# Head gates packed into three recurrent weight tiles, and two groups of steps placed a chunk later

## The chip, the cores and the metric

The kernel runs on one core of one Trainium2 chip. The metric is device microseconds of one launch, all weights being read from HBM; the median of three runs before the change is 1436.12 us (1435.93 to 1438.66).

## The reference

Two layers of a first block (hybrid mixer, memory cross attention, convolutional feed-forward) and then one layer of a second block run over 256 tokens of width 1024, in fp32. The change touches the second block alone, in its first part:

```python
xn = rmsnorm(x, norm_mix)
(u_rnn, u_gate, q, k_c, v_c, k_s, v_s, k_w, v_w, g_nsa, g_a, g_b) = jnp.split(xn @ w_in, cuts, axis=-1)
h_a = rg_lru(causal_depthwise_conv(u_rnn, conv_w, conv_b), gate_a_w, ...)   # 1344 channels, 4 gate blocks of 336
y_a = h_a * jax.nn.gelu(u_gate, approximate=True)
y_b = nsa_mixer(q, k_c, v_c, k_s, v_s, k_w, v_w, g_nsa, ...)
#   kc = rmsnorm(compress_blocks(k_c)); vc = compress_blocks(v_c)   (pe added, then gelu(flat @ w1) @ w2)
#   gates = sigmoid(g_nsa): 16 heads x 3;  o = g0 * o_c + g1 * o_s + g2 * o_w
merged = sigmoid(g_a) * (y_a @ proj_a) + sigmoid(g_b) * (y_b @ proj_b)
h = x + merged @ w_out
return h + square(relu(rmsnorm(h, norm_mlp) @ w_mlp_in)) @ w_mlp_out
```

`g_nsa` is a product of the 1024 features with 48 columns. `u_rnn` and `u_gate` have 1344 columns each.

## The kernel before, in words

Activations lie feature-major in SBUF: `fmh` and `fml` hold the high and the low part of an fp32 value, split so that a product runs as three fp32r matmuls (high by high, low by high, high by low). A weight tile is one DMA of up to 128x1024 elements into `raw`; ScalarE casts it to `wh` (L220) and VectorE subtracts for `wl` (L221). `Stream.take` hands out the tiles in a fixed order (`order2`), issues loads ahead on SP's queue, and splits two tiles ahead; tiles named `pkv` are used as they are, unsplit. There are four `raw` buffers and four of each of `wh` and `wl`.

A chunk is one weight tile. `mm_a` multiplies its eight 128-row parts with the 256 tokens: 24 matmuls (L410 to L412) into one PSUM tile of pool `mm`, which has four. The recurrent stage (`lru_steps`) walks four blocks: three chunks `ur` of 112 output columns with a convolution after each (kind "u"), three of `ug` with a gelu (kind "g"), and the block's two gates `lga` and `lgx`, each one tile with three groups of nine matmuls, 27 in all (kind "b"). After the two gates of a block, `lru_tail` does the scan in five pieces.

The order on TensorE is the program's order. On the other engines a scheduler lays out the instructions with priorities; each engine then runs its queue in order. Work beside the chunks is tied to ticks: every `take` is a tick (`tick`, L349), `later(n, fn)` runs a function n ticks on, and generators in `back` go one step a tick.

Around the change, `block2` first makes the queries and the keys `k2` and `v2`. `put_ks` (L1533) turns the normalised keys of two token halves, two kinds each, by four transposes into a PSUM tile of pool `tp`, which has two; ScalarE and VectorE split the result into `ks` (L1529, L1530). Then come four chunks `cc`, whose results are copied alternately by ScalarE and VectorE into two tiles `zt` (L1555) and completed by a sum with the position values (L1557, on VectorE). Then the chunk `gn`, the head gates, with its 48 columns padded to 128; ScalarE copies it out (L1562), and two ticks later `gates` transposes it (L1567).

The compressed keys are `phi_steps`: eight `pkv` steps, one between any two recurrent chunks, each with eight fp32 matmuls on both `zt` tiles (L1215); then, one step a tick, a gelu, transposes, copies, a second product, a norm (`kc_ss`, `rstd` on GpSimd, L1254) and a transpose (L1258). After the last, `nsa_units` starts: 16 attention units with score matmuls, VectorE reductions (L1398 to L1411), six ScalarE exponentials (L1417), transposes and sums, the first four units five ticks apart and the others two. They run beside the recurrent blocks and the merge gates `ga`, `pa`, `gb`.

Of the kernel before, what the change touches and what calls it, by code (L numbers as in the profile page):

```python
# [15 lines left out]
AF = mybir.ActivationFunctionType  # L16
# [3 lines left out]
S = 256  # L20
D = 1024
# [5 lines left out]
RW = 112  # L27
# [105 lines left out]
def layout2(f, o):  # L133
    g = {k[:-2]: v[0] for k, v in f.items() if k.endswith("_2") and v.ndim > 1 and v.shape[0] == 1}
    w = g["w_in"]
    cut = np.cumsum([0, 1344, 1344, 1024] + [256] * 6 + [48, 1024, 1024])
    ur, ug, q, kc, vc, ks, vs, kw, vw, gn, ga, gb = (w[:, i:j] for i, j in zip(cut[:-1], cut[1:]))
    o["ur"], o["ug"] = pack_a(ur, RW), pack_a(ug, RW)
    o["q2"] = pack_b(q)
    o["k2"] = pack_b(np.concatenate([ks, kw], 1))  # L140
    o["v2"] = pack_b(np.concatenate([vs, vw], 1))
    o["cc"] = pack_a(np.concatenate([kc, vc], 1))
    o["gn"] = pack_a(np.pad(gn.reshape(D, 16, 3)[:, :, [1, 2, 0]].transpose(0, 2, 1).reshape(D, 48), ((0, 0), (0, 80))))
    o["ga"], o["gb"] = pack_a(ga), pack_a(gb)
    for key, name in (("lga", "gate_a_w"), ("lgx", "gate_x_w")):
        o[key] = np.concatenate([pack_a(g[name][b], RW, RW, 9) for b in range(4)])
    o["pa"] = pack_a(g["proj_a"], 128, RW, 6)
    o["pb"] = pack_a(g["proj_b"])
    o["wo2"] = pack_b(g["w_out"])
    o["minb"], o["min"] = pack_b(g["w_mlp_in"][:, :512]), pack_a(g["w_mlp_in"][:, 512:])  # L150
    o["mout"] = pack_b(g["w_mlp_out"])
    w1 = np.stack([g[n].reshape(8, 2, 128, 256) for n in ("phi_k_w1", "phi_v_w1")], 1)
    o["pkv"] = np.ascontiguousarray(w1.transpose(0, 3, 1, 2, 4).reshape(8, 128, 1024))
    w2 = np.stack([g["phi_k_w2"], g["phi_v_w2"]])
    o["phi2"] = np.ascontiguousarray(w2.reshape(2, 2, 128, 64).transpose(2, 0, 1, 3))
    pe = [g[n].reshape(16, 2, 64).transpose(1, 2, 0).reshape(128, 16) for n in ("phi_k_pe", "phi_v_pe")]
    two = [np.tile(g[n], 2)[:, None] for n in ("q_norm", "ks_norm", "kw_norm")]
    o["feat2"] = np.ascontiguousarray(np.concatenate(two + pe, 1))
    o["rnn"] = np.ascontiguousarray(np.concatenate(
        [feat(g["conv_w"], RW).reshape(RW, -1)] + [feat(g[n].reshape(-1), RW) for n in  # L160
                                                   ("conv_b", "gate_a_b", "gate_x_b", "lru_lambda")], 1))
    o["kcg"] = g["kc_norm"]
    o["nmix"], o["nmlp"] = g["norm_mix"], g["norm_mlp"]
    rb = np.concatenate([f["rel_bias_2"], np.full((1, 16), NEG, np.float32)])
    p = np.arange(128)[:, None]
    dist = 128 + p - np.arange(256)[None]
    idx = np.where(dist >= 0, _bucket(dist), 32)
    o["tbias"] = np.ascontiguousarray(rb[idx].transpose(0, 2, 1))
    dc = p[:, :, None] + 128 * np.arange(2)[None, :, None] - (16 * np.arange(15) + 31)[None, None]
    o["cbias"] = np.ascontiguousarray(rb[np.where(dc >= 0, _bucket(dc), 32)].transpose(0, 1, 3, 2))  # L170
    o["cval"] = (p >= 31).astype(np.float32)
# [84 lines left out]
class Program:  # L256
# [50 lines left out]

    def order2(self, add):
        add("q2", len(EARLY))
        for key in ("k2", "v2", "cc", "gn"):  # L310
            add(key)
        n = 0
        for kind, b in LRU_ORDER:
            for i in range(2 if kind == "b" else 3):
                if kind == "b":
                    add("lgx" if i else "lga", b, b + 1)
                else:
                    add("ur" if kind == "u" else "ug", 3 * b + i, 3 * b + i + 1)
                if n < 8:
                    add("pkv", n, n + 1)  # L320
                n += 1
        for key in ("ga", "pa", "gb", "pb", "wo2", "minb", "min", "mout"):
            add(key)
# [955 lines left out]
        nc.vector.scalar_tensor_tensor(cl, cl, -4.0, sr, op0=OP.mult, op1=OP.add)  # L1279
        nc.vector.tensor_scalar(rp[:, 5 * RT:7 * RT], rp[:, 5 * RT:7 * RT], 0.5, None, op0=OP.mult)  # L1280

    def lru_steps(self, xs, ya, pool, prm):


        nc, w = self.nc, self.w
        cw, cb, ba, bx, cl = prm
        xcs = {}
        for kind, b in LRU_ORDER:
            if kind == "u":
                xc = xcs[b] = pool.tile([RW, 3, S], F32, name="xc", bufs=2)  # L1290
                for i in range(3):
                    n = 3 * b + i
                    ps = self.mm((128, S))
                    self.mm_a(ps[:RW], w.take("ur"), self.fmk(xs), nw=RW)
                    nc.scalar.activation(xc[:, i], ps[:RW], AF.Identity, bias=cb[:, n:n + 1],
                                         scale=cw[:, 3 * RT + n:3 * RT + n + 1])
                    for s in (1, 2, 3):
                        nc.vector.scalar_tensor_tensor(xc[:, i, s:], ps[:RW, :S - s],
                                                       cw[:, (3 - s) * RT + n:(3 - s) * RT + n + 1], xc[:, i, s:],
                                                       op0=OP.mult, op1=OP.add)  # L1300
                    yield
                xh = pool.tile([RW, 3, S], F32R, name="xch", bufs=1)
                xl = pool.tile([RW, 3, S], F32R, name="xcl", bufs=1)
                self.split(xh, xl, xc)
                continue
            if kind == "g":
                ug = self.yp.tile([RW, 3, S], F32, name="ug", tag=f"yah{b}", bufs=1)
                for i in range(3):
                    ps = self.mm((128, S))
# [165 lines left out]
    def block2(self, x, xs, outs):  # L1475
        nc, tc, w, a = self.nc, self.tc, self.w, self.a
        with ExitStack() as st:
# [54 lines left out]

            def put_ks(t, kn):  # L1533
                for i in range(2):
                    self.later(2 + i, partial(put_k, kn, t, i))

            self.spawn(self.head_norm([out.rearrange("p (h d) -> p h d", d=64) for out in outs], 8, self.sm, put_ks,
                                      True))
# [4 lines left out]
            for kind in range(2):  # L1543
# [12 lines left out]
                pe = fp[:, 3 + 16 * kind:19 + 16 * kind]  # L1556
                nc.vector.tensor_add(zt, zt, pe[:, :, None].to_broadcast([128, 16, 60]))  # L1557
                zts.append(zt)
            ps = self.mm((128, S))
            self.mm_a(ps, w.take("gn"), self.fmk(xs))  # L1560
            gs = self.k2((48, S))
            nc.scalar.copy(gs, ps[:48])  # L1562

            def gates():
                for t in range(2):
                    tp = self.tp((128, 48))
                    nc.tensor.transpose(tp, gs[:, t * 128:t * 128 + 128], self.ident[:48, :48])  # L1567
                    gv = gt[:, t].rearrange("p b h -> p (b h)")
                    nc.scalar.activation(gv, tp, AF.Tanh, scale=0.5)
                    nc.vector.tensor_scalar(gv, gv, 0.5, 0.5, op0=OP.mult, op1=OP.add)  # L1570
                nc.vector.tensor_scalar(gt[:, 0, 2], gt[:, 0, 2], cval, None, op0=OP.mult)

            self.later(2, gates)

            ya, self.yp = [], pool
            yb = self.fm()
# [3 lines left out]
            self.back.append(self.attend(self.nsa_units(qt, ks, v, vcz, gt, pcs, yb), *NSA))  # L1580
            with tc.tile_pool(name="lru", bufs=1) as lp:
                prm = rp[:, :4 * RT], rp[:, 4 * RT:5 * RT], rp[:, 5 * RT:6 * RT], rp[:, 6 * RT:7 * RT], cl
                for i, _ in enumerate(self.lru_steps(xs, ya, lp, prm)):
                    if i < 8:
                        next(phi)
                    elif i == 8:
                        self.back.append(phi)
                for g in self.back:
                    if g.gi_code.co_name == "lru_tail":
# [92 lines left out]
```

## Time and profile before

| what | us |
|---|---|
| median of three runs | 1436.12 |
| profiled execution | 1439.39 |
| its span, first to last instruction | 1437.6 |
| TensorE busy | 1415.7 (98%) |
| VectorE busy | 1083.4 (75%) |
| ScalarE busy | 891.7 (62%) |

Matmuls are pipelined: their recorded durations overlap, and what one costs in a row of equal ones is the distance between two starts. A wait is a gap before an instruction, put down to what ended it. Line numbers are those of the kernel before; in the changed file the same lines stand 2 to 10 lines further down.

### The profile page before, as it was taken

Reading aid. Unit: us, or ns where it says so; the run is one execution under the profiler, and the core shown is the slowest. Engines: PE = TensorE matmul, PEld = TensorE weight load, DVE = VectorE, ACT = ScalarE, POOL = GpSimd, SP = SyncE. Lnnn points to the kernel's source line nnn. Section 1 sums busy time; section 2 is a strip of 40 time slices with the busy share of each in tenths; the row PEclk is TensorE's granted clock in tenths of the full one; section 3 lists DMA queues with packets and bytes.
Section 4 is the critical chain, followed back from the end, with each engine's and each line's share of the span. In section 5 each row is a group of like instructions: output and inputs, shape, how many; then the busy total and the mean of one; then the engine's idle time right before and its main releaser. Section 6 shows DMA issues by size and latency. Waiting matters only on the chain.

```text
span 1437.6 us, 26028 instructions
## 1 busy us (share of the span) xinstructions
PE 1415.7 (98%) x9919; PEld 1289.7 (90%) x9919; DVE 1083.4 (75%) x2196; ACT 891.7 (62%) x1609; POOL 47.0 (3%) x143
## 2 busy tenths in 40 slices
PE   8999999999999999999999999999999999999998
PEld 6899988899988899998889998788989999899987
DVE  6997676788857898668679986786789785866543
ACT  5876556666645486655667665464898775555432
POOL 1110000000000020000000000120100000000000
PEclk9999999999999999999999999999999999999999
DMA  8454564555556544455636557356544445645563
GB/s 316 166 191 148 191 220 136 187 187 192 182 193 218 180 152 152 137 204 175 220 132 213 196 198 260 110 171 190 167 131 142 133 145 176 208 154 197 191 206 103
DMA packets 75335, 257.63 MB, mean 179 GB/s; under 512 B 9803, under 2 KB 11211, under 8 KB 75083
## 3 DMA queue, kind: packets, MB, share of 16 engines
q1 hardware_dynamic: 75211, 255.97, 54.3%
q8 instruction: 78, 1.28, 0.3%
q14 instruction: 46, 0.38, 0.1%
HBM read 254.89 MB, written 1.05 MB: 178 GB/s over the span
## 4 chain that ended last, share of the span: by engine, by line
PE 83%; DVE 6%; ACT 5%; DMA 3%; issue 1%; POOL 1%; SPq 0%; DVEq 0%; ACTq 0%; POOLq 0%
PE mm L410 16%; PE mm L411 15%; PE mm L412 15%; PE mm L426 8%; PE mm L424 8%; PE mm L425 8%; DVE wl L221 2%; PE mm L467 2%; PE mm L469 2%; PE mm L470 2%; ACT wh L220 1%; PE tp L772 1%; PE tp L733 1%; DMA raw<-in_kv_dram 1%; PE sc L695 1%
## 5 line engine op out<-in xcount | busy, mean ns | idle before, releaser
L220 ACT CAST wh<-raw 128x1024 fp32r<-128x1024 f32 (+3 forms) x432 | 446.5, 1038 | 373.0 <-PE mm L411 124.4
L221 DVE TENSOR_TENSOR wl<-raw,wh 128x1024 fp32r<-128x1024 f32 (+3 forms) x432 | 518.0, 1204 | 210.8 <-ACT wh L220 202.3
L410 PE MATMUL mm<-fmh,wh 128*128 128x256 f32 (+1 forms) x1736 | 487.0, 281 | 2.8 <-ACT macc L1599 1.5
L412 PE MATMUL mm<-fmh,wl 128*128 128x256 f32 (+1 forms) x1736 | 483.5, 278 | 0.0
L411 PE MATMUL mm<-fml,wh 128*128 128x256 f32 (+1 forms) x1736 | 483.4, 278 | 0.0
L410 PEld LDWEIGHTS mm<-fmh,wh 128*128 128x128 f32 (+1 forms) x1736 | 324.9, 187 | 8.1 <-issue 2.9
L412 PEld LDWEIGHTS mm<-fmh,wl 128*128 128x128 f32 (+1 forms) x1736 | 324.5, 187 | 0.0
L411 PEld LDWEIGHTS mm<-fml,wh 128*128 128x128 f32 (+1 forms) x1736 | 323.7, 186 | 0.2
L424 PE MATMUL mm<-wh,fmh 128*128 128x512 f32 x200 | 79.7, 398 | 2.0 <-ACT wh L220 1.3
L425 PE MATMUL mm<-wl,fmh 128*128 128x512 f32 x200 | 78.6, 393 | 0.8 <-DVE wl L221 0.8
L426 PE MATMUL mm<-wh,fml 128*128 128x512 f32 x200 | 78.8, 394 | 0.0
L425 PE MATMUL mm<-wl,ah 128*128 128x512 f32 x164 | 63.8, 389 | 0.0
L426 PE MATMUL mm<-wh,al 128*128 128x512 f32 x164 | 63.8, 389 | 0.0
L424 PE MATMUL mm<-wh,ah 128*128 128x512 f32 x164 | 63.8, 389 | 0.0
L410 PE MATMUL mm<-oh,wh 128*128 128x256 f32 x192 | 54.1, 282 | 0.0
L412 PE MATMUL mm<-oh,wl 128*128 128x256 f32 x192 | 53.5, 279 | 0.0
L411 PE MATMUL mm<-ol,wh 128*128 128x256 f32 x192 | 53.5, 279 | 0.0
L425 PE MATMUL mm<-wl,zh 128*128 128x512 f32 x128 | 49.8, 389 | 0.0
L424 PE MATMUL mm<-wh,zh 128*128 128x512 f32 x128 | 49.8, 389 | 0.0
L426 PE MATMUL mm<-wh,zl 128*128 128x512 f32 x128 | 49.8, 389 | 0.0
L1086 ACT ACTIVATE k<-mm,featp 128x256 f32<-128x256 f32 x88 | 48.5, 558 | 0.0
L424 PEld LDWEIGHTS mm<-wh,fmh 128*128 128x128 f32 x200 | 37.6, 188 | 10.1 <-ACT wh L220 1.8
(406 smaller groups left out, 2638.3 us busy)
## 6 DMA issues: line engine op xcount, KB each, us to landing
raw<-in_up_dram SPq DMA_DIRECT2D x80, 512.0 KB, 4.3
raw<-in_gate_dram SPq DMA_DIRECT2D x48, 512.0 KB, 3.5
raw<-in_down_dram SPq DMA_DIRECT2D x44, 512.0 KB, 4.3
raw<-in_mout_dram SPq DMA_DIRECT2D x32, 512.0 KB, 4.3
raw<-in_min_dram SPq DMA_DIRECT2D x28, 512.0 KB, 4.3
raw<-in_br_dram SPq DMA_DIRECT2D x24, 512.0 KB, 3.6
raw<-in_mix_dram SPq DMA_DIRECT2D x16, 512.0 KB, 3.7
raw<-in_wo_dram SPq DMA_DIRECT2D x16, 512.0 KB, 3.5
```

The source lines that it names most:

```text
L220: self.nc.scalar.copy(h[:p, :w], r[:p, :w])
L221: self.last = self.nc.vector.tensor_sub(l[:p, :w], r[:p, :w], h[:p, :w].bitcast(F32))
L410: self.nc.tensor.matmul(ps, wh[:kw, c], xh[k], start=start and k == 0, stop=False)
L411: self.nc.tensor.matmul(ps, wh[:kw, c], xl[k], start=False, stop=False)
L412: self.nc.tensor.matmul(ps, wl[:kw, c], xh[k], start=False, stop=stop and k == n - 1)
L424: self.nc.tensor.matmul(outs[t], xh[:, k, r], wh[:, c], start=k == 0, stop=False)
L425: self.nc.tensor.matmul(outs[t], xh[:, k, r], wl[:, c], start=False, stop=False)
L426: self.nc.tensor.matmul(outs[t], xl[:, k, r], wh[:, c], start=False, stop=k == k_all - 1)
L467: self.nc.tensor.matmul(outs[t], xl[:, k, r], wh, start=False, stop=k == 7)
L469: self.nc.tensor.matmul(outs[t], xh[:, k, r], wh, start=k == 0, stop=False)
L470: self.nc.tensor.matmul(outs[t], xh[:, k, r], wl, start=False, stop=False)
L1086: nc.scalar.activation(y[:, i], ps, AF.Identity, bias=cb[:, c:c + 1], scale=k[1])
```

## The change

The 48 gate columns are cut into three groups of 16 and put behind the 112 columns of the first three `ur` tiles, which become 128 columns wide under the key `ur0`; the tile `gn` and its product are gone. After each of these three products ScalarE copies PSUM rows 96 to 127 into a third of `gs` (16 rows of it are unused), and `gates` transposes 96 rows at once. `gates` is called two ticks behind the third chunk. The `pkv` steps begin behind the second recurrent chunk instead of the first, and what follows them is as much later. The two kinds of keys of one token half are transposed two ticks apart instead of one.

```diff
-    o["ur"], o["ug"] = pack_a(ur, RW), pack_a(ug, RW)
+    gn = gn.reshape(D, 16, 3)[:, :, [1, 2, 0]].transpose(0, 2, 1)
+    first = np.concatenate([ur[:, :3 * RW].reshape(D, 3, RW), gn], 2).reshape(D, 384)
+    o["ur0"], o["ur"], o["ug"] = pack_a(first), pack_a(ur[:, 3 * RW:], RW), pack_a(ug, RW)
...
-        for key in ("k2", "v2", "cc", "gn"):
+        for key in ("k2", "v2", "cc"):
             add(key)
...
-                if n < 8:
-                    add("pkv", n, n + 1)
+                if 0 < n < 9:
+                    add("pkv", n - 1, n)
...
-                    self.mm_a(ps[:RW], w.take("ur"), self.fmk(xs), nw=RW)
+                    if b:
+                        self.mm_a(ps[:RW], w.take("ur"), self.fmk(xs), nw=RW)
+                    else:
+                        self.mm_a(ps, w.take("ur0"), self.fmk(xs))
+                        nc.scalar.copy(gs[32 * i:32 * i + 32], ps[96:])
...
+                if not b:
+                    self.later(2, gates)
...
-                    self.later(2 + i, partial(put_k, kn, t, i))
+                    self.later(2 + 2 * i, partial(put_k, kn, t, i))
...
-            ps = self.mm((128, S))
-            self.mm_a(ps, w.take("gn"), self.fmk(xs))
-            gs = self.k2((48, S))
-            nc.scalar.copy(gs, ps[:48])
+            gs = self.k2((96, S))
...
-                for i, _ in enumerate(self.lru_steps(xs, ya, lp, prm)):
-                    if i < 8:
+                for i, _ in enumerate(self.lru_steps(xs, ya, lp, prm, gs, gates)):
+                    if 0 < i < 9:
                         next(phi)
-                    elif i == 8:
+                    elif i == 9:
                         self.back.append(phi)
```

Three places where instructions change their order follow. The first is VectorE's queue from the third `cc` chunk to the second `zt` sum. `k_11145` and `k_11227` are the two `zt` tiles, `ks` the split keys. Before:

```order
L221 TENSOR_TENSOR wl<-raw,wh 128x896
L1277 SCALAR_TENSOR_TENSOR sp_10994<-sp_10994,sp_10992 112x12
L1530 SCALAR_TENSOR_TENSOR ks_10848<-tp,fp_10833,ks_10847 128x4x128
L1279 SCALAR_TENSOR_TENSOR cl<-cl,sp_10994 112x12
L1555 COPY k_11145<-mm 64x16x15
L1530 SCALAR_TENSOR_TENSOR ks_10848<-tp,fp_10833,ks_10847 128x4x128
L1557 TENSOR_TENSOR k_11145<-k_11145,fp_10833 128x960
L1555 COPY k_11227<-mm 64x16x15
L1530 SCALAR_TENSOR_TENSOR ks_10848<-tp,fp_10833,ks_10847 128x4x128
L1555 COPY k_11227<-mm 64x16x15
L221 TENSOR_TENSOR wl<-raw,wh 128x896 x2
L1555 COPY k_11227<-mm 64x16x15 x2
```

The next row there is the second sum, L1557. Now, down to the same sum:

```order
L1540 SCALAR_TENSOR_TENSOR ks_10848<-tp,fp_10833,ks_10847 128x4x128
L1283 SCALAR_TENSOR_TENSOR cl<-cl,sp_10994 112x12
L1565 COPY k_11145<-mm 64x16x15
L1567 TENSOR_TENSOR k_11145<-k_11145,fp_10833 128x960
L1565 COPY k_11227<-mm 64x16x15
L1540 SCALAR_TENSOR_TENSOR ks_10848<-tp,fp_10833,ks_10847 128x4x128
L1565 COPY k_11227<-mm 64x16x15
L223 TENSOR_TENSOR wl<-raw,wh 128x1024
L223 TENSOR_TENSOR wl<-raw,wh 128x896
L1565 COPY k_11227<-mm 64x16x15
L1540 SCALAR_TENSOR_TENSOR ks_10848<-tp,fp_10833,ks_10847 128x4x128
L1565 COPY k_11227<-mm 64x16x15
```

The last key split has moved between the last two copies, and the two weight splits before those copies are the third `ur0` tile and the first `ug` tile instead of the second and third `ur`.

The second place is SP's queue, from the tile behind the last `cc`. Before:

```order
L193 DMA raw<-in_gn_dram 128x1024
L193 DMA raw<-in_ur_dram 128x896
L193 DMA raw<-in_pkv_dram 128x1024
L193 DMA raw<-in_ur_dram 128x896
L193 DMA raw<-in_pkv_dram 128x1024
L193 DMA raw<-in_ur_dram 128x896
L193 DMA raw<-in_pkv_dram 128x1024
L193 DMA raw<-in_ug_dram 128x896
```

Now:

```order
L195 DMA raw<-in_ur_dram 128x1024 x2
L195 DMA raw<-in_pkv_dram 128x1024
L195 DMA raw<-in_ur_dram 128x1024
L195 DMA raw<-in_pkv_dram 128x1024
L195 DMA raw<-in_ug_dram 128x896
```

Each recurrent tile has moved one place up, so that the first `ug` stands where the last `ur` of the first block stood.

The third place is ScalarE's queue in the third recurrent block, at the second attention unit. `lga` is the first gate's tanh (L1328) and later its tail, `k,ns` and `pc,ns` are the exponentials. Before:

```order
L1315 ACTIVATE k_12298<-k_12298 112x256
L1313 ACTIVATE k_12413<-mm 112x256
L220 CAST wh<-raw 128x896
L1417 ACTIVATE k_12312,ns<-k_12312,nm 128x256
L1417 ACTIVATE k_12313,ns<-k_12313,nm 128x256
L1417 ACTIVATE pc_10854,ns<-pc_10854,nm 128x15
L1417 ACTIVATE k_12312,ns<-k_12312,nm 128x256
L1417 ACTIVATE k_12313,ns<-k_12313,nm 128x256
L1417 ACTIVATE pc_10854,ns<-pc_10854,nm 128x15
L1315 ACTIVATE k_12377<-k_12377 112x256
L1315 ACTIVATE k_12413<-k_12413 112x256
L1328 ACTIVATE lga<-mm,rp_10835 112x256 x2
```

Now:

```order
L1325 ACTIVATE k_12259<-k_12259 112x256
L222 CAST wh<-raw 128x896
L1323 ACTIVATE k_12384<-mm 112x256
L1338 ACTIVATE lga<-mm,rp_10835 112x256
L1350 ACTIVATE al<-lga,cl 112x256
L1325 ACTIVATE k_12310<-k_12310 112x256
L1355 ACTIVATE lga<-lga,cl 112x256
L1338 ACTIVATE lga<-mm,rp_10835 112x256
L1350 ACTIVATE al<-lga,cl 112x256
L1338 ACTIVATE lga<-mm,rp_10835 112x256
L1427 ACTIVATE k_12324,ns<-k_12324,nm 128x256
L1427 ACTIVATE k_12325,ns<-k_12325,nm 128x256
```

The three tanh of the gate `lga`, which read `mm` tiles, now stand before the six exponentials; the three of `lgx` still stand behind them.

## Rows read from the trace of the kernel before

**Rows 1.** Windows: start:end us, length, busy us (instructions) per engine, clock, DMA, GB/s.
```profile
961.40:982.00 20.60, 19.13 (x163) 18.50 (x162) 19.06 (x37) 10.90 (x19) 1.20 (x2) 1.00 0.51 159
...
1021.00:1059.00 38.00, 36.49 (x308) 35.86 (x305) 35.90 (x89) 31.94 (x64) 4.57 (x12) 1.00 0.39 127
1059.00:1120.00 61.00, 56.11 (x473) 53.69 (x474) 53.68 (x153) 55.35 (x129) 0.00 (x0) 1.00 0.46 147
1120.00:1210.00 90.00, 90.00 (x776) 84.84 (x775) 65.55 (x286) 64.91 (x210) 0.00 (x0) 1.00 0.48 147
```

**Rows 2.** Chain of waits in order of time, 950 to 1125 us: start, us, what.
```profile
972.19 0.67 DVE ks L1530
...
1012.62 0.46 ACT lgx L1328
...
1113.71 0.39 ACT macc L1599
```

**Rows 3.** TensorE's waits, 930 to 1240 us: total, times, longest.
```profile
PE mm L410 <- ACT lga L1328: 1.6, 1, 1.6
PE mm L410 <- ACT macc L1599: 1.5, 1, 1.5
PE tp L1526 <- DVE ks L1530: 1.5, 2, 0.9
PE tp L1258 <- DVE k L1254: 1.1, 1, 1.1
PE mm L410 <- DVE nm L1411: 0.9, 1, 0.9
PE mm L412 <- DVE wl L221: 0.7, 1, 0.7
PE tp L1244 <- DVE k L1232: 0.4, 1, 0.4
```

**Rows 4.** Timeline of TensorE, 976 to 983 us: start, us, instruction.
```profile
976.13 0.28 PE L410 MATMUL mm<-fmh,wh 128*128 128x256 f32 x1
...
978.85 0.28 PE L410 MATMUL mm<-fmh,wh 128*112 128x256 f32 x1
...
981.76 0.32 PE L1567 MATMUL tp<-ident,k 48*128 48x48 f32 x2
982.01 1.08 PE L1215 MATMUL sc<-raw,k 128*60 128x256 f32 x8
```

**Rows 5.** Timeline of VectorE, 968 to 983 us.
```profile
969.17 1.22 DVE L221 TENSOR_TENSOR wl<-raw,wh 128x1024 fp32r<-128x1024 f32 x1
...
979.85 0.41 DVE L1555 COPY k<-mm 64x240 f32<-64x240 f32 x1 [0.42 <-ACT k L1555]
980.29 1.16 DVE L1557 TENSOR_TENSOR k<-k,fp 128x960 f32<-128x960 f32 x1
```

**Rows 6.** Groups by line and form, 961.3 to 982.1 us: busy us, mean ns.
```profile
L221 DVE TENSOR_TENSOR wl<-raw,wh 128x1024 fp32r<-128x1024 f32 x3 | 3.6, 1217 | 0.0
...
L221 DVE TENSOR_TENSOR wl<-raw,wh 128x896 fp32r<-128x896 f32 x3 | 3.2, 1087 | 0.0
```

**Rows 7.** Groups by form of TensorE's weight loads, 961.3 to 982.1 us.
```profile
L411 PEld LDWEIGHTS mm<-fml,wh 128*128 128x128 f32 x40 | 7.5, 188 | 0.0
...
L410 PEld LDWEIGHTS mm<-fmh,wh 128*112 128x112 f32 x8 | 1.4, 175 | 0.0
```

**Rows 8.** Timeline of SP's queue, 940 to 1040 us: DMA issues.
```profile
972.17 0.33 SPq L193 DMA_DIRECT2D raw<-in_ur_dram  x1
...
979.02 0.33 SPq L193 DMA_DIRECT2D raw<-in_ug_dram  x1
```

**Rows 9.** DMA issues by line: count, KB each, median us to landing.
```profile
raw<-in_ug_dram SPq DMA_DIRECT2D x12, 448.0 KB, 3.7
```

**Rows 10.** Timeline of ScalarE, 1061 to 1066 us.
```profile
1061.04 0.51 ACT L1417 ACTIVATE k<-k,nm 128x256 f32<-128x256 f32 x1
...
1063.61 0.71 ACT L1315 ACTIVATE k<-k 112x256 f32<-112x256 f32 x2
```

More of the change, by code (lines that the diff above doesn't have):

```diff
@@ L142, in layout2 @@
     o["cc"] = pack_a(np.concatenate([kc, vc], 1))
-    o["gn"] = pack_a(np.pad(gn.reshape(D, 16, 3)[:, :, [1, 2, 0]].transpose(0, 2, 1).reshape(D, 48), ((0, 0), (0, 80))))
     o["ga"], o["gb"] = pack_a(ga), pack_a(gb)
@@ L316, in order2 @@
                     add("lgx" if i else "lga", b, b + 1)
-                else:
-                    add("ur" if kind == "u" else "ug", 3 * b + i, 3 * b + i + 1)
-                if n < 8:
-                    add("pkv", n, n + 1)
+                elif kind == "u":
+                    add("ur" if b else "ur0", 3 * max(b - 1, 0) + i, 3 * max(b - 1, 0) + i + 1)
+                else:
+                    add("ug", 3 * b + i, 3 * b + i + 1)
+                if 0 < n < 9:
+                    add("pkv", n - 1, n)
                 n += 1
@@ L1280, in lru_rate, with lru_steps @@
         nc.vector.tensor_scalar(rp[:, 5 * RT:7 * RT], rp[:, 5 * RT:7 * RT], 0.5, None, op0=OP.mult)
-    def lru_steps(self, xs, ya, pool, prm):
+    def lru_steps(self, xs, ya, pool, prm, gs, gates):
         nc, w = self.nc, self.w
@@ L1558, in block2 @@
                 zts.append(zt)
-            ps = self.mm((128, S))
-            self.mm_a(ps, w.take("gn"), self.fmk(xs))
-            gs = self.k2((48, S))
-            nc.scalar.copy(gs, ps[:48])
+            gs = self.k2((96, S))
             def gates():
                 for t in range(2):
[L1566 to L1569, printed above, removed]
+                    tp = self.tp((128, 3, 32))
+                    nc.tensor.transpose(tp.rearrange("p b h -> p (b h)"), gs[:, t * 128:t * 128 + 128],
+                                        self.ident[:96, :96])
+                    gv = gt[:, t]
+                    nc.scalar.activation(gv, tp[:, :, 16:], AF.Tanh, scale=0.5)
                     nc.vector.tensor_scalar(gv, gv, 0.5, 0.5, op0=OP.mult, op1=OP.add)
                 nc.vector.tensor_scalar(gt[:, 0, 2], gt[:, 0, 2], cval, None, op0=OP.mult)
-            self.later(2, gates)
             ya, self.yp = [], pool
```

## The prediction

> **What bounds the kernel now.** I read the page first, then the windows around the edited stretch, then the chain of waits in order of time, then TensorE's waits, and last the timelines of single engines. TensorE runs at the full granted clock throughout, and where it is busy without a gap a matmul taken out is worth its time. But the edit lies in the part of the program where this is least true. The windows show it: from 961.4 to 982.0 VectorE is busy 19.06 of 20.60 us, while TensorE stands still for about 1.5; from 1021 to 1059 VectorE has 35.90 of 38; from 1059 to 1120 ScalarE has 55.35 of 61 and TensorE loses 4.9; from 1120 on TensorE is busy without a gap [rows 1]. The chain says the same: up to 972.9 it is VectorE's, ending with a key split; then TensorE's, until pieces of ScalarE and VectorE set in at 1012.62; the last ScalarE piece before the stretch without gaps is a merge gate's tanh at 1113.71 [rows 2]. The waits to look for: key transposes 1.5 us, compressed keys 1.1 and 0.4, third block of the recurrent stage 1.6, 0.9 and 0.7, and 1.5 at the start of the merge gates [rows 3].
>
> **The removed chunk.** The head gates' own product is 24 matmuls, from 976.13 to the first recurrent matmul at 978.85: 2.72 us [rows 4]. In its place the first three recurrent chunks have 128 stationary columns instead of 112, and still 24 matmuls each. Their cost is bounded from rows at either width: the 24 of the 128-wide chunk took 2.72 us, those of the 112-wide chunk behind it 2.91, from 978.85 to 981.76, with a change to another kind of matmul at its end [rows 4]. So a wider tile costs between -0.2 and +0.2 us a chunk, and I take 0. Its weight loads do get longer, 188 against 175 ns mean [rows 7], but matmuls of the wide chunk start every 0.113 us, so the recorded loads overlap and do not add up on the path.
>
> The Trainium skill has a rule that speaks against this edit ("TensorE: Matmul & The Clock Gate", section "LDWEIGHTS (loading the stationary operand)"): a load's time goes with its columns, 1/1.2 ns each. By it 72 loads of 16 more columns are an estimated 0.96 us, if loads set the pace, and the forecast would be later by that much; the trace agrees that wider loads are longer, and its chunk of wide loads is not slower.
>
> ScalarE copies 32x256 three times instead of 48x256 once. Two more copies, each at most the 0.51 us of a 128x256 exponential [rows 10], are up to 1.0 us on an engine that is busy 10.90 of 20.60 us there [rows 1]. That idle time covers them; without it they cost that 1.0. The two gate transposes (0.25 us, 981.76 to 982.01 [rows 4]) stay, three chunks later.
>
> **Up to the first step of the compressed keys.** Today the key transposes wait 1.5 us for VectorE to empty their PSUM tile [rows 3], since two sets of them stand side by side and the pool has two tiles. A chunk apart they find a free one. Between the first set and the first `pkv` step stand six chunks now as before (four of `cc`, then two of the recurrent stage instead of the head gates' and one), so TensorE comes to `pkv` at 982.01 less the gate transposes' 0.25 and the waits' 1.5: 980.3. But `pkv` needs both summed `zt` tiles, and the second sum is VectorE's. Its queue is full from 969.17 to that sum's end at 981.45 (980.29 + 1.16), but for the 0.42 us before 979.85 [rows 5]. The new order of that queue holds, over the same stretch, the same copies, key splits and sums, but three weight splits of 1024 columns and one of 896, where there were one and three; at 1217 and 1087 ns this adds 0.26 us [rows 6]. A key split now stands between the two last copies, so that the gap of 0.42 fills. The sum then ends at 981.45 + 0.26 - 0.42 = 981.29, and `pkv` starts at about 981.35 instead of 982.01: -0.66 us. So the wait of the keys is not won as a whole: some 1.0 us of it is late again, in one piece, at the first `pkv` matmul. Bounds: -1.7 (VectorE is never late) and +0.4 (the gap stays and the queue is late by as much again).
>
> **Behind it.** From the first `pkv` step to the chunk behind the last one there are seven recurrent chunks instead of eight, with the same `pkv` steps between them: -2.72, and +0.25 for the gate transposes, which now stand here: -2.47. The chain gives this stretch to TensorE until about 1012 [rows 2].
>
> **The moved steps.** The compressed keys and then every attention unit run one recurrent chunk later against the recurrent work. No row shows that alignment, so I bound it. At best all waits of that part go: 1.6 + 1.5 + 1.1 + 0.9 + 0.7 + 0.4 = 6.2 us [rows 3]. At worst one more burst of six exponentials (1061.04 to 1063.61, 2.57 us [rows 10]) stands before a tanh that TensorE waits for: +2.6. Between these I go place by place. The 1.1 and 0.4 of the compressed keys should go: the path through ScalarE's square, VectorE's start of the reciprocal root, GpSimd's steps and the scaling is covered by two chunks of 24 matmuls and one of 27 instead of three of 24, and VectorE's start stands further forward in its queue: -1.5. In the third block the new ScalarE order puts the tanh of the first gate ahead of the six exponentials and leaves those of the second gate behind them: the 3.2 us there become perhaps 2.2: -1.0. At the merge gates one more chunk asks for a PSUM tile before the same tanh: +1.2. Together -1.3.
>
> **DMA.** SP issues one load fewer, and each load stands one recurrent tile earlier in its queue. The tile `ug` takes the place of the last `ur` of the first block, issued at 972.17 [rows 8]; with 3.7 us to landing [rows 9] it is there at 975.9. VectorE wants its split at 981.29 less the work behind it: 1.09 + 0.41 + 0.67 + 0.41 + 1.16 [rows 2, 5, 6], at 977.6. No cost taken.
>
> **Sum.** -0.66 - 2.47 - 1.3 = -4.4 us. The profiled execution took 1439.39 us (span 1437.6), 3.3 above the median of 1436.12; it would fall to about 1435.0, and the median to 1431.7. About 0.2%, 2.9 us, is what a measurement here can tell from no change.
>
> **The rivals.** *The middle stretch takes it back.* ScalarE and VectorE set the time between 1012 and 1114, and what TensorE does not do comes back as waits. For it: their shares of 88 to 94% [rows 1], and the chain. Against: their inputs come from recurrent chunks that come earlier, and their own work does not grow. Then -0.66 and little of the chunk remain, about -1.2: 1434.9. *The waits go too.* Those of the compressed keys and all three of the third block (1.5 + 3.2) go, and the merge gates are no worse: -0.66 - 2.47 - 4.7 = -7.8: 1428.3. For it: the attention units meet one recurrent chunk less, and the stretch from 1120 has room on both engines [rows 1]; against: the exponentials still stand before some tanh. *Slower: a weight split in front of the copies.* In the new VectorE order the split of the first `ug` tile stands ahead of the last two copies that the `zt` sum needs, and the queue is in order: if that tile lands late, the first `pkv` waits with it. In the kernel before, `ug` was issued at 979.02 [rows 8]; 3.7 us to landing and about 1 us of ScalarE's cast (near the split's 1.09) put the split at 983.7, 6.1 us after VectorE wants it. That gives +6.1 - 4.4 = +1.7: 1437.8, and 1439.1 if the -1.3 fails too. It decides from the point where `ug` lands after 976.6. Against it: its new place in SP's queue.
>
> **How the numbers follow.** Forecast 0.57 (its own range 1429.8 to 1433.6), middle stretch 0.20, waits go 0.17, slower 0.06. The range of 8 in 10 runs from 1428.6 to 1434.9. Faster by over 0.2% means below 1433.25: nearly all of the forecast (0.53), all of the third case (0.17), a part of the second (0.05): 0.75. Within 0.2%: 0.18. Slower: 0.07.
>
> **What would show it.** TensorE has no wait at the key transposes, and one of about 1 us for VectorE's sum at the first `pkv` matmul, which starts some 0.7 us before 982.0; the last `pkv` step ends about 3 us earlier than now; the wait before the compressed keys' transpose is below 0.4; the third block has one wait for a tanh that stands behind exponentials. Wrong would be: a `pkv` start later than 982.0, a wait for a DMA of `ug` in VectorE's or ScalarE's queue before it, or more than 7 us of TensorE waits between 1012 and 1120.

## The result, and the profile after

The changed kernel is slower. Its median is 1445.71 us (1443.48 to 1451.46, six runs) against 1436.80 us (1435.87 to 1440.05, six runs) of the kernel before: ratio 1.0057, 95% interval 1.0036 to 1.0078. Twelve more runs later give 1445.32 against 1439.11 us, ratio 1.0044 (1.0028 to 1.0060). The forecast was 1431.7.

The profiled execution has a span of 1442.8 us, 5.2 more than before. Up to the first `cc` chunk both traces run alike (961.22 and 961.44 us); from there to the first transposes behind the block it is 300.22 us instead of 294.59. I call this the block's length. The windows of the changed kernel where the clock column changes:

```profile
982.00:984.50 2.50, 2.27 (x13) 1.78 (x14) 1.53 (x4) 0.85 (x1) 0.00 (x0) 0.79 0.33 104
984.50:987.00 2.50, 2.50 (x14) 2.50 (x14) 2.31 (x4) 1.02 (x3) 0.00 (x0) 0.53 0.62 216
...
1113.00:1115.50 2.50, 0.09 (x1) 0.09 (x1) 2.03 (x3) 1.59 (x3) 0.00 (x0) 0.53 0.19 45
1115.50:1118.00 2.50, 2.50 (x12) 2.50 (x13) 0.00 (x0) 2.50 (x14) 0.00 (x0) 0.50 0.30 114
1118.00:1120.50 2.50, 2.50 (x15) 2.50 (x15) 1.51 (x8) 0.31 (x3) 0.00 (x0) 0.60 0.00 0
```

The first column behind the length is TensorE, the third from the right the granted clock. Twice it falls to half, 1.2 instead of 2.4 GHz, and TensorE is "busy" there while it does 12 to 15 matmuls in 2.5 us instead of 22 to 24. In [rows 1] it is 1.00 everywhere. TensorE's waits, to be held against [rows 3]:

```profile
PE mm L414 <- ACT macc L1605: 4.2, 1, 4.2
PE sc L1219 <- DVE k L1567: 1.9, 1, 1.9
PE tp L1248 <- DVE k L1236: 1.3, 1, 1.3
PE mm L414 <- ACT pct L1455: 1.1, 2, 0.9
PE mm L414 <- DVE xc L1306: 0.8, 2, 0.7
PE mm L414 <- DVE ug L1326: 0.7, 2, 0.4
PE mm L414 <- ACT lga L1338: 0.6, 1, 0.6
PE mm L414 <- ACT lgx L1338: 0.6, 1, 0.6
PE tp L1240 <- DVE k L1232: 0.5, 1, 0.5
```

The first fall comes behind the second longest of these waits, the second within the longest. TensorE's timeline at both places (the first `pkv` step stands at 982.01 in [rows 4]):

```profile
979.70 0.64 PE L1219 MATMUL sc<-raw,k 128*60 128x256 f32 x2
982.23 1.04 PE L1219 MATMUL sc<-raw,k 128*60 128x256 f32 x6 [1.89 <-DVE k L1567]
983.21 0.40 PE L414 MATMUL mm<-fmh,wh 128*128 128x256 f32 x1
...
987.73 1.08 PE L1219 MATMUL sc<-raw,k 128*60 128x256 f32 x8
...
1115.41 0.58 PE L414 MATMUL mm<-fmh,wh 128*128 128x256 f32 x1 [4.20 <-ACT macc L1605]
...
1120.38 0.59 PE L1460 MATMUL tp<-pct,vcz 128*128 128x256 f32 x2
```

The chunk behind the first pause takes 987.73 - 983.21 = 4.5 us, where a later such pair, at full clock, stands 3.0 apart (992.93 to 995.92); the fifth chunk of the merge gate `ga` takes 1120.38 - 1115.41 = 5.0. The same chunk in the kernel before, where it waits 1.5 us:

```profile
1111.15 1.52 PE L1454 MATMUL tp<-k,v 128*64 128x128 f32 x16
1114.15 0.38 PE L410 MATMUL mm<-fmh,wh 128*128 128x256 f32 x1 [1.48 <-ACT macc L1599]
...
1116.98 0.29 PE L695 MATMUL sc<-ks,qt 128*128 128x272 f32 x1
```

That is 2.8 us. So the falls cost 1.5 and 2.1 us beside the pauses.

Why is VectorE's second `zt` sum late? Its timeline, to be held against [rows 5], then GpSimd's two rows, then one row of each in the kernel before:

```profile
971.31 0.99 DVE L1280 TENSOR_SCALAR sp<-sp 112x12 f32<-112x12 f32 x1
...
980.93 1.16 DVE L1567 TENSOR_TENSOR k<-k,fp 128x960 f32<-128x960 f32 x1
```

```profile
971.06 0.96 POOL L1234 MEMSET k<- 128x1024 f32 x1 [14.29 <-PE tp L1536]
971.96 0.31 POOL L1223 MEMSET k<- 128x256 f32 x1
```

```profile
968.10 0.95 POOL L1230 MEMSET k<- 128x1024 f32 x1 [11.14 <-PE tp L1526]
...
969.09 0.24 DVE L1276 TENSOR_SCALAR sp<-sp 112x12 f32<-112x12 f32 x1
```

The sum ends at 982.09, not at 981.29. Nearly all of these 0.80 us is one tiny VectorE instruction: 0.99 us, and it ends with GpSimd's memsets, which clear tiles for the compressed keys. Elsewhere the same line takes 0.17. Before, the memsets began at 968.10 and met that line for 0.07 us only. Their tile is freed by the key transposes, and spreading these moved it. The Trainium skill ("SBUF — State Buffer", section "SBUF: two separate sides") has VectorE and GpSimd share a pair of ports under an exclusive lock, and the one that comes second is blocked for the whole instruction of the first. Of VectorE's operations it names those in a two-port mode, and those with two SBUF inputs only against a GpSimd operation that reads SBUF. The rows agree: the memset reads nothing, and the weight split that runs when it starts (970.17), with two inputs, keeps its 1.22 us.

Why does the merge gate wait 4.2 instead of 1.5 us? The fifth chunk needs a PSUM tile, which the first `macc` tanh frees; `macc` lies in the memory of the recurrent stage and waits for its last subtraction, `yal`. VectorE, then ScalarE, then VectorE in the kernel before:

```profile
1109.84 1.20 DVE L223 TENSOR_TENSOR wl<-raw,wh 128x1024 fp32r<-128x1024 f32 x1
1110.96 0.95 DVE L1367 SCALAR_TENSOR_TENSOR lga<-lga,ug 112x768 f32<-112x768 f32 x1
...
1112.86 1.22 DVE L223 TENSOR_TENSOR wl<-raw,wh 128x1024 fp32r<-128x1024 f32 x1
1113.99 0.95 DVE L401 TENSOR_TENSOR yal<-lga,yah 112x768 fp32r<-112x768 f32 x1
```

```profile
1114.98 0.94 ACT L1605 ACTIVATE macc<-mm 128x256 f32<-128x256 f32 x3 [0.91 <-DVE yal L401]
```

```profile
1111.48 0.96 DVE L397 TENSOR_TENSOR yal<-lga,yah 112x768 fp32r<-112x768 f32 x1
...
1112.43 3.49 DVE L221 TENSOR_TENSOR wl<-raw,wh 128x1024 fp32r<-128x1024 f32 x3
```

Two weight splits now stand ahead of `yal`, beside an attention unit's maxima, which stood there before as well; before, the splits came behind it. The tanh comes at 1114.98 instead of 1113.71 [rows 2]. And TensorE is early: the sums of an attention unit, 2 us of work which stood ahead of the fifth chunk before (up to the end of the row at 1111.15), now come one chunk later.

### The profile page after: what moved, and what is told of

Read it like the earlier page. It is cut to its first block, busy times and chain, and to the rows that moved or that the text cites. A ratio compares the mean times of both kernels' runs of the same rounds, so it can differ in the third digit from the quotient of the medians.

```text
span 1442.8 us, 25992 instructions
## 1 busy us (share of the span) xinstructions
PE 1419.1 (98%) x9895; PEld 1292.4 (90%) x9895; DVE 1084.7 (75%) x2195; ACT 892.2 (62%) x1610; POOL 47.8 (3%) x143
## 4 chain that ended last, share of the span: by engine, by line
PE 82%; DVE 7%; ACT 5%; DMA 3%; issue 2%; POOL 1%; SPq 0%; DVEq 0%; ACTq 0%
PE mm L414 15%; PE mm L415 15%; PE mm L416 15%; PE mm L428 8%; PE mm L430 8%; PE mm L429 8%; DVE wl L223 2%; PE mm L471 2%; PE mm L473 2%; PE mm L474 2%; ACT wh L222 1%; PE tp L776 1%; PE tp L737 1%; DMA raw<-in_kv_dram 1%; PE tp L1464 1%
## 5 line engine op out<-in xcount | busy, mean ns | idle before, releaser
L430 PEld LDWEIGHTS mm<-wh,fml 128*128 128x128 f32 x200 | 37.6, 188 | 8.5 <-DVE fml L1003 0.2
```

The source lines that it names most:

```text
L430: self.nc.tensor.matmul(outs[t], xl[:, k, r], wh[:, c], start=False, stop=k == k_all - 1)
```

## The experiments

Theory A: the later steps (part b of the change: `pkv`, compressed keys and attention units one recurrent chunk later) lay the waits anew, the memset makes the first one longer, and pauses let the clock fall. Rivals: the packed tiles cost; the spread of executions; late weights. For each run the median and the ratio to before, the mean granted clock of all its executions, then of its one trace the block's length and where in the block the clock falls ("gate" is the fifth chunk of `ga`):

| run | median, ratio (95%) | mean clock | block us | clock falls at |
|---|---|---|---|---|
| before | | 0.998 | 294.6 | nowhere |
| changed | 1445.7, 1.0057 (1.0036-1.0078) | 0.996 | 300.2 | first `pkv`, gate |
| changed, again | 1445.3, 1.0044 (1.0028-1.0060) | 0.996 | 299.6 | first `pkv`, gate |
| memsets late, new tile | 1450.1, 1.0070 (1.0050-1.0089) | 0.997 | 296.3 | gate |
| memsets late | 1441.9, 1.0013 (0.9996-1.0030) | 0.997 | 299.2 | compressed keys, gate |
| memset twice | 1442.5, 1.0029 (1.0012-1.0047) | 0.996 | 302.0 | compressed keys, gate |
| filler | 1439.7, 1.0015 (0.9998-1.0031) | 0.998 | 297.4 | first `pkv` |
| units back | 1441.5, 1.0005 (0.9988-1.0021) | 0.996 | 299.3 | compressed keys, third block |
| before + b | 1445.3, 1.0047 (1.0027-1.0067) | 0.996 | 302.7 | compressed keys, gate |
| b undone | 1443.2, 1.0014 (0.9998-1.0030) | 0.997 | 297.0 | first `pkv`, third block |
| keys undone | 1443.2, 1.0022 (1.0005-1.0039) | 0.997 | 296.9 | gate |
| before + keys | 1438.5, 0.9989 (0.9969-1.0010) | 0.999 | 295.5 | third block |
| before, mended | 1440.2, 1.0004 (0.9983-1.0025) | 0.999 | 293.7 | nowhere |
| changed, mended | 1436.3, 0.9973 (0.9957-0.9988) | 1.000 | 292.4 | nowhere |

A trace is one execution, and the clock differs between executions. The kernel before is not free of falls: in the series beside "changed, again" six of its 35 executions have a mean of 1.000, the lowest 0.996. All 18 executions of the changed kernel lie between 0.994 and 0.998, and of the twelve of "changed, mended" eleven have 1.000. The means of that one series are 0.9959 for the changed kernel and 0.9983 for the kernel before. The difference over 1440 us is 3.5 us of the 6.2 between their medians: an estimate, as if TensorE had been busy all the time.

The kernel before has medians from 1436.1 to 1440.7 us in four series of runs, and the pace of matmuls in stages that no edit touches differs between traces (last section); the block's length doesn't contain these stages. Within the block, 256-wide matmuls that follow each other at full clock start 116.8 to 117.1 ns apart on average in every trace but one: in that of the first memset trial they start 116.0 ns apart, which makes its block an estimated 1 us shorter, its slower 512-wide matmuls counted in.

**The changed kernel again.**

> The changed kernel once more, unaltered, with more timed executions beside the kernel before. Theory A (two stalls of over 2 us let TensorE's clock fall): the trace again has a wait of 4.2 us before the fifth merge-gate chunk with the clock down to 0.5 behind it, and one more fall either at the first pkv step (wait 1.9) or at the compressed keys' transposes (waits 0.5 and 1.3); the time is 4 to 8 us above the kernel before. Rival B (the slower time of the first measurement was mostly the spread between executions that have the 118 ns and those that have the 113 ns pitch of matmuls in unchanged stages): within 0.2% of the kernel before.

Waits of 1.75 us (first `pkv`) and 4.2 us (gate), and clocks of 0.76 and 0.73 in the 5 us windows that hold them. Theory A; the spread alone is excluded, since the interval stays above 1.

**Part b alone.** On the kernel before:

```diff
-                if n < 8:
-                    add("pkv", n, n + 1)
+                if 0 < n < 9:
+                    add("pkv", n - 1, n)
...
-                    if i < 8:
+                    if 0 < i < 9:
```

> The kernel before, with one part of the change alone: the pkv steps, and with them the compressed keys and all attention units, one recurrent chunk later; the head gates' own chunk and the key transposes as before. Theory A (the moved units lay the waits anew): the merge gates' wait is about 4 us instead of 1.5 with a fall of the clock behind it, the compressed keys' waits are 1.8 instead of 1.5, the first pkv step has no wait (VectorE's sum ends at 981.5, TensorE comes at 984.7): 3 to 5 us slower than before. Rival B (the loss belongs to the packed tiles or the removed chunk): within 1 us of before.

```profile
PE mm L410 <- ACT macc L1599: 4.2, 1, 4.2
...
PE tp L1244 <- DVE k L1232: 1.3, 1, 1.3
```

With nothing packed and nothing removed, the gate's wait and the longer one of the compressed keys are those of the changed kernel. Part b costs 302.7 - 294.6 = 8.1 us of block, more than the 3 to 5 expected; the clock falls at two places where one was expected. The two other parts take 2.5 to 3.1 us off again, about the removed chunk's 2.7. So b alone costs as much as the whole change, by the block and by the median (1.0047 against 1.0044).

**Part b undone.** On the changed kernel, the same lines the other way.

> The changed kernel with the pkv steps (and with them the compressed keys and all attention units) one recurrent chunk earlier again, as in the kernel before; packed gate columns and spread key transposes stay. Lengths are taken from the first cc chunk to the first transposes behind the block: 294.6 us before, 300.2 and 299.6 in the two traces of the changed kernel. Theory A (the removed chunk was cover for VectorE's second zt sum, and the later steps are what costs): TensorE comes to the first pkv step near 977 and waits until about 981 for the sum, a pause of about 4 us with a fall of the clock behind it; behind that all waits are those of before (compressed keys 1.5, third block 3.2, merge gates 1.5): 295.5 to 297. Rival B (the removed chunk is worth its 2.7 us wherever the steps stand): 292.

```profile
PE sc L1219 <- DVE k L1567: 3.5, 1, 3.5
PE mm L414 <- ACT lga L1338: 1.6, 1, 1.6
PE mm L414 <- ACT macc L1605: 1.6, 1, 1.6
```

The gate's wait is back at 1.6. The chunk behind the first `pkv` step starts 21.5 us after the first `cc` chunk, in the kernel before 21.6: the removed chunk comes back whole as a wait for VectorE's sum. Without b the change wins nothing either: that chunk was cover. The block is 2.4 us longer than that of the kernel before, with falls at the first `pkv` and in the third block; by the median no difference to the kernel before is shown.

**Units back.** `NSA = (4,) + (5,) * 3 + (2,) * 12, 4, 2` in the changed kernel.

> The changed kernel, with the attention units from the second on one recurrent chunk earlier (the first unit's distance 4 ticks instead of 5), which is how they stood against the recurrent chunks in the kernel before. Theory A (the wait of 4.2 us before the fifth merge-gate chunk is long because no attention sums stand before it any more and because VectorE and ScalarE meet another unit's work in front of the last recurrent outputs): that wait is about 1.5 us again, the clock stays 1.00 from 1110 to 1120, the fifth chunk takes 2.7 us instead of 5.0; the third block's waits return to about 3.2 from 2.3. Net 2.7 + 2.3 - 0.9 = 4.1 us less than the changed kernel: profiled span near 1438.7, median near 1441.6. Rival B (the wait comes from the order of the weight splits, which the removed chunk shifts, and not from the units): no change, wait still above 3.5 us, clock still near 0.5 to 0.8 there.

```profile
PE sc L1219 <- DVE k L1567: 1.7, 1, 1.7
PE mm L414 <- ACT macc L1605: 1.6, 1, 1.6
```

The wait is the units' alignment, as theory A has it, and the clock stays up at the gate. But the block is only 0.3 to 0.9 us shorter than the changed kernel's: the third block's waits return, and the clock falls at the compressed keys (0.66 over 1020 to 1030) and in the third block (0.69 over 1060 to 1070).

**Filler.** Transposes that nobody reads, ahead of the fifth gate chunk:

```diff
+                wt = w.take("ga")
+                if n == 4:
+                    fill = self.tp((128, 128))
+                    for _ in range(36):
+                        nc.tensor.transpose(fill, self.ident, self.ident)
```

> The changed kernel, with 36 more transposes of the identity (about 3.3 us of TensorE work at 0.09 us each, into a PSUM tile that nobody reads) in front of the fifth merge-gate chunk, where TensorE waits 4.2 us. Theory A (the chunk behind the wait takes 5.0 instead of 2.7 us because the clock fell while TensorE stood still): the chunk starts when it did, the clock stays 1.00 from 1110 to 1120, the chunk takes 2.7 us, and the span falls by about 2.3 us to 1440.5 (median 1443.4) although work was added. Rival B (the chunk is slow because its weights or its PSUM tile are late): no gain, 1442.8. Rival C (the added transposes cost their time): plus up to 3.3.

```profile
1108.50:1111.00 2.50, 2.23 (x20) 1.99 (x19) 1.82 (x3) 1.60 (x4) 0.00 (x0) 1.00 0.27 54
1111.00:1113.50 2.50, 2.50 (x23) 2.50 (x23) 0.00 (x0) 2.50 (x14) 0.00 (x0) 1.00 0.26 99
```

The clock stays at 1.00, the chunk takes 2.9 us, and with 36 transposes more the block is 2.2 to 2.8 us shorter, as expected (2.3). So the price behind the pause is the clock's.

**Memsets late, twice.** In the first trial a one-element operation with a tile of its own:

```diff
+        late = self.sm.tile([128, 1], F32, name="late")
+        self.zt_done = nc.gpsimd.tensor_scalar(late, zts[1][:, 0, :1], -0.5, 1.5, op0=OP.mult, op1=OP.add)
...
+        with tc.issue_after(self.zt_done.ins):
+            nc.gpsimd.memset(hid, 0.0)
```

> The changed kernel, but GpSimd's two memsets for the compressed keys stand behind a one-element GpSimd operation that reads the second summed zt tile, so they start after about 982 us instead of at 971.06. Theory A (the memsets hold a VectorE tensor_scalar for 0.82 us, the sum and the first pkv step come that much later, and the stall of 2.3 us that results lets TensorE's clock fall): the tensor_scalar takes 0.17 us again, the sum ends near 981.3, the wait at the first pkv step falls from 1.9 to about 1.1, the granted clock stays 1.00 from 980 to 990, and the chunk behind the step takes 3.0 us instead of 4.5: 0.8 + 1.5 = 2.3 us less than the changed kernel, a profiled span near 1440.5 and a median near 1443.4. Rival B (the clock falls for another reason than the length of this stall): only 0.8 us less, clock still near 0.81 there. Rival C (the 0.99 us of the tensor_scalar has nothing to do with GpSimd): no change, 1445.7.

In the second the operation writes into `hid` itself.

> The changed kernel with GpSimd's two memsets behind the second zt sum, this time without a new SBUF tile (the one-element operation writes into the tile that the memset then clears), so that all tiles stand where they do in the changed kernel. Theory A: the tensor_scalar takes 0.17 us, the wait at the first pkv step is 1.2 instead of 1.9, no fall of the clock there, and the 512-wide matmuls of the unchanged stages start every 227 ns as in the changed kernel (233 in the earlier trial, which had moved all tiles by 4 bytes): 0.8 us less than the changed kernel, and 1.5 more where that has its clock fall at this place. Rival B (the 233 ns came by chance and not from the tiles' place): 233 ns may return or not, in stages that the edit doesn't touch.

VectorE's row in the second:

```profile
971.80 0.16 DVE L1282 TENSOR_SCALAR sp<-sp 112x12 f32<-112x12 f32 x1
```

In both the wait is 1.2 us and the clock holds at the first `pkv`, as theory A has it. That the shorter wait is why is not shown, since the clock held behind 1.75 us in two other traces. And in the second it falls a little further on, behind the compressed keys' waits of 0.3 and 1.3 (0.69 over 1022 to 1027), so the block wins only 0.5 to 1.1 us and not 2.3. The first trial was 4 us slower than the changed kernel for another reason. One row each of the 512-wide matmuls far ahead of the block, of before, the first and the second trial:

```profile
420.00:440.00 20.00, 20.00 (x90) 16.57 (x89) 10.84 (x14) 8.82 (x12) 0.00 (x0) 1.00 0.59 198
```

```profile
420.00:440.00 20.00, 20.00 (x87) 16.14 (x86) 9.98 (x13) 9.13 (x12) 0.00 (x0) 1.00 0.61 184
```

```profile
420.00:440.00 20.00, 20.00 (x90) 16.57 (x89) 10.80 (x14) 8.86 (x12) 0.00 (x0) 1.00 0.59 190
```

The tile of 4 bytes is the only thing in memory that tells the two trials apart; with it 87 matmuls run in 20 us, without it 90. Chance (rival B) fits badly: the fastest of the first trial's six executions took 1446.31 us, the slowest of the second's twelve 1445.79. That the place of the tiles is the cause, and not something else in the build, is not shown.

**Memset twice.** `nc.gpsimd.memset(hv, 0.0)` written two times.

> The changed kernel with the larger of the two GpSimd memsets (128x1024) done twice. Theory A (VectorE's tensor_scalar waits until GpSimd's memsets end): the tensor_scalar takes about 1.9 us instead of 0.99, the second zt sum ends near 983.0, the stall at the first pkv step grows from 2.3 to 3.2 us, the clock falls at least as far, span plus 0.9 to 2 us (1443.7 to 1444.8). Rival B (no link between the two): unchanged, 1442.8.

```profile
966.73 0.83 DVE L1281 TENSOR_SCALAR sp<-sp 112x12 f32<-112x12 f32 x1
```

```profile
966.57 0.96 POOL L1234 MEMSET k<- 128x1024 f32 x1 [14.38 <-PE tp L1537]
967.59 0.96 POOL L1235 MEMSET k<- 128x1024 f32 x1
```

Theory A's number failed: the instruction gets its turn between the two memsets, which stand 0.06 us apart (967.53 to 967.59). It waits for the one that runs, not for GpSimd to be idle; in the changed kernel the two memsets leave no gap, and it waits for both. Nor did the clock fall at the first `pkv` behind its wait of 1.74 us; it fell at the compressed keys and at the gate, and the block is the longest of the changed kernel's variants.

**Key transposes.** Put back in the changed kernel (`later(2 + i, ...)`):

> The changed kernel with the key transposes at 2 and 3 ticks again, as before (two sets side by side); packed columns and later steps stay. Theory A (the spread transposes free the memsets' tile later, which is why the memset meets VectorE's tensor_scalar): the memset runs some 3 us earlier, no tensor_scalar of over 0.3 us, the key transposes wait 1.5 us again, the first pkv step waits under 0.6 us; the merge gates still wait 4.2 us with a fall of the clock. Length 298 to 299.5 us from the first cc chunk, that is, spreading the transposes gained nothing. Rival B (the spread is worth its 1.5 us): 301.5.

```profile
PE mm L414 <- ACT macc L1605: 4.1, 1, 4.1
PE tp L1536 <- DVE ks L1540: 1.6, 2, 1.0
```

The keys wait 1.6 us, the first `pkv` not at all, and only the gate's fall is left: 296.9, shorter than expected. The memset now runs 3.2 us earlier and draws one instruction out to 0.23 us only. So in the changed kernel the spreading only gathered two short waits (0.6 and 1.0 us) into one long one. Spread in the kernel before (`later(2 + 2 * i, ...)`):

> The kernel before with only the key transposes spread (2 and 4 ticks). Theory A: their 1.5 us of waits go and come back at the first pkv step, where TensorE is now 1.5 us early and waits for VectorE's sum, 0.7 us longer still if the memset meets the tensor_scalar; length 294.6 us from the first cc chunk as before, plus up to 1.5 if the clock falls. Rival B (the waits are won): 293.1.

Here 1.0 of the 1.5 us is won, against theory A: the wait at the first `pkv` is 0.5, and the memset (970.21) meets no such instruction. A fall in the third block (0.83 over 1060 to 1070) takes it back. The block lies in theory A's range, but by a fall at another place than it meant.

**Mended.** The changed kernel with late memsets, and:

```diff
-        nc.vector.tensor_copy(ht, tp[:, :, :60])
+        with self.tc.high_priority(offset=100):
+            nc.vector.tensor_copy(ht, tp[:, :, :60])
...
+                if n == 4:
+                    w.hold((tail, first))
+                wt = w.take("ga")
+                if n == 4:
+                    fill = self.tp((128, 128))
+                    for _ in range(16):
+                        nc.tensor.transpose(fill, self.ident, self.ident)
```

The copies into `hv` have the higher priority too; `tail` is the last recurrent subtraction, `first` the first `macc` tanh, and `hold` puts the next two weight splits behind them.

> The changed kernel with four edits: GpSimd's memsets behind the second zt sum; VectorE's copies for the compressed keys at a higher priority (ahead of a weight split and the first block's last subtraction); the casts and splits of merge-gate weights 6 and 7 behind the first merge-gate tanh and the last recurrent output, so that these come first; 16 transposes of the identity before the fifth merge-gate chunk. Theory A: no fall of the clock in the block; the wait before the fifth chunk 4.2 to about 0.7 behind the 16 transposes (macc's tanh at 2 us earlier), the compressed keys' waits 1.8 to 0.5, the first pkv wait 1.9 to 1.2. Against the changed kernel 0.7 + 1.5 + 1.3 + 2.0 + 2.3 = 7.8 us less, about 2 us under the kernel before. Rival B (VectorE and ScalarE bound the stretch, so what one wait loses another gains): at most 4.5 us less than the changed kernel, level with or above the kernel before.

```profile
PE sc L1219 <- DVE k L1571: 1.1, 1, 1.1
PE mm L414 <- ACT pct L1459: 1.0, 2, 0.9
```

```profile
957.94:1250.32 292.38, 286.79 (x2322) 267.39 (x2322) 231.13 (x653) 213.81 (x497) 6.33 (x15) 1.00 0.50 163
```

No wait above 1.1 us, the clock at 1.00 through the block, 7.3 to 7.8 us less than the changed kernel, as theory A has it, and a version faster than both kernels. The same copies and `hold` in the kernel before:

> The kernel before with two of the four mends that made the changed kernel faster: VectorE's copies for the compressed keys at a higher priority, and the casts and splits of merge-gate weights 6 and 7 behind the first merge-gate tanh and the last recurrent output (there is no clock fall to fill and no memset to move here). Theory A (the packed gate columns keep a part of their 2.7 us once their new waits are mended): compressed keys' first wait 0.45 to 0, merge gates' 1.5 to about 0.5, length 293.2 us, so that the mended changed kernel (292.4) stays under it by about 1 us. Rival B (all of the mended kernel's gain comes from the mends): 292.4 or less.

293.7, and a ratio of 1.0004. In one trace of each, both without a fall, the mended changed kernel is 1.3 us shorter in the block, about half of the removed chunk's 2.7. It has two mends that this one lacks, and a wait of 1.6 us at the compressed keys' norm stands here that it doesn't have; so how much of the chunk is kept is not settled, and the intervals of the two ratios still touch.

## Why the prediction was wrong, step by step

- **What bounds the kernel now.** "TensorE runs at the full granted clock throughout" is true of the profiled execution of before, but not of most others (0.998 on average). I carried it over to a kernel with longer pauses and gave no rival a fall. The falls cost 1.5 + 2.1 us in the first trace. This is the missing term.
- **The removed chunk.** Right as work: 24 matmuls are gone, and the wide tiles cost nothing (from 975.87 to 979.27 thirty matmuls start, 0.113 us each). That the time is won too holds only where no other engine is late: with b undone the 2.7 us come back as a wait. No run has the packed tiles alone.
- **Up to the first `pkv`.** The wait was named, 1.0 us, and is 1.9. TensorE arrives at 979.70, 0.6 earlier than reckoned; VectorE's queue was counted right but for one instruction, which the memset holds up for 0.8. I had looked past GpSimd, whose memset hangs on the tile that the moved transposes free. -0.66 became +0.2 at the chunk behind the step (983.21 against 983.02).
- **Behind it.** The seven chunks are right. The chain was misread: from 1007.63 to 1011.75 it names a load of `ur`, not TensorE, which had no gap there. The test named for it was wrong by count: the last `pkv` step stands one chunk later in the order and could not end 3 us earlier. It starts 1.8 later (1012.73 against 1010.89), of which 1.5 is the fall.
- **The moved steps** failed. Compressed keys: -1.5 forecast, +0.3 measured (0.5 + 1.3 against 0.4 + 1.1). The 1.1 behind the norm did go, as reasoned, but the waits for VectorE's copies grew from 0.4 to 1.8, because the first block's scan and last product (1018.31 to 1021.16) now stand ahead of these. Third block: 3.2 to 2.3 (its waits for `xc`, `ug`, `lga`, `lgx`), near the 2.2 forecast. Merge gates: +1.2 forecast, +2.7 measured, and 1.1 more at `ug` and `pct` ahead of it. Sum -1.3 forecast, +3.2 measured, over its upper bound of +2.6 even without the clock. This is the term that turned the sign: "one more chunk asks for a PSUM tile" was priced, but not the two weight splits ahead of `yal` nor the sums that no longer stand before the wait.
- **DMA.** Right: no wait before the first `pkv` is one for `ug`.
- **The rivals.** The middle stretch did take it back, but that case ended at -1.2 since it reckoned no loss. The slower rival was the wrong mechanism.

Together: the listed waits are 11.7 us against 7.7 in [rows 3], +4.0; the chunk is -2.7, the falls +3.6: +4.9 of the 5.6 us by which the block grew. The rest is not traced. Two of the signs that I had named for being wrong came: the `pkv` matmuls that need the second sum start at 982.23, later than 982.0, and the waits between 1012 and 1120 are 9.8 us, more than 7.

## What to carry to other kernels

Work on the bounding engine that is another engine's cover can be worth nothing when removed: ask first who would be late next, through every engine, GpSimd's memsets and the tiles they wait for included. When steps tied to ticks move by one chunk, look for the place where TensorE waits for a freed tile and see which work stood ahead of that wait. A pause near 2 us can cost nearly as much again if the clock falls behind it: 1.5 us behind 1.9 here. Two waits of 0.6 and 1.0 us were cheaper than one of 1.9 (key transposes), though falls stood behind two short waits too. Read the granted clock of all executions, not of the profiled one alone.

## What the runs showed of the hardware

- TensorE's granted clock fell from 2.4 to 1.2 GHz at the gate in all seven traces with a wait of 4.1 or 4.2 us there. At the first `pkv` step it fell behind waits of 1.75, 1.9 and 3.5 us, at the compressed keys behind 0.2 or 0.3 and 1.3 us close together, and in the third block behind 0.9, 0.7 and 1.6 us or four of 0.5 to 1.0. It held in other traces with the same waits: 1.75 us at the first `pkv` ("units back", "memset twice"), 0.5 and 1.3 (the changed kernel), the third block of before. In no trace did it fall at the first `pkv` and at the compressed keys both. What decides is open.
- With one tile of 4 bytes more, matmuls in stages that the edit doesn't touch ran at another pace: 87 instead of 90 in 20 us, and 1450.1 against 1441.9 us in the median. Whether the place of the tiles does that, and how, is open.
- Between 320 and 340 us, far from all edits, 256-wide chunks ran at two paces: 173 matmuls in the second trace of the changed kernel and 178 in the filler's, both at full clock, with the same tiles and code there. The cause is open; it is why the block's length was compared.
